# Two output blocks of a decoder layer as seven block products, with the weight sums formed in memory by DMA

## The chip, the cores and the metric

The kernel runs on one core of one Trainium2 chip. The metric is device time of one execution in microseconds (us); the time of a kernel is the median of its runs. A profile is of one execution, and its span is somewhat shorter than that execution's time.

The core has a matrix engine (TensorE, PE in the profile; its weight loads are listed as PEld), a vector engine (VectorE, DVE), a scalar engine (ScalarE, ACT), a general engine (GpSimd, POOL) and a sync engine (SP) that issues DMAs. PE reads on-chip buffers and writes accumulators in PSUM, of which there are eight banks of 128 x 512 float32. DMAs move data between the memory outside the core and the buffers, and also from one place of that memory to another; those that POOL issues can add to what lies at their destination.

## The reference, cut to what matters

One layer of a hybrid decoder, float32, 256 tokens of width 2048, one batch:

```python
h = rms_norm(x, ln1_g)
proj = h @ w_in                                   # 2048 x 14416, cut into twelve parts
o_attn = dsa_attention(...)                       # sparse attention over the top 64 keys
o_ret = silu(rg) * group_norm_heads(retention)    # retention branch, its output gated
merged = sigmoid(ga) * (o_attn @ w_up_attn) + sigmoid(gb) * (o_ret @ w_up_ret)
x = x + merged @ w_out                            # all four of these matrices 2048 wide
h2 = rms_norm(x, ln2_g)
x = x + square(relu(h2 @ w_ff1)) @ w_ff2          # 2048 -> 8192 -> 2048
```

The change concerns `merged @ w_out`: 256 x 2048 by 2048 x 2048.

## The kernel before, in words

**Precision.** PE multiplies in a reduced float32 format. Every operand is therefore split in two, a rounded high part and the low rest, and each product is three matmuls: high by high, high by low, low by high (`products`, L438, L439, L440). For weights the split is made on the fly: ACT copies the raw tile to the high part `whi` (L379), DVE subtracts to get the low part `wlo` (L380).

**Tiles.** The 256 tokens are two row tiles (T = 2) of 128. The contraction of 2048 is 16 tiles of 128. A weight matrix is worked in column blocks of 512 (BN). A plain block is 16 x 2 x 3 = 96 matmuls into two PSUM banks, and is called by its name: UR0 to UR3 (`w_up_ret`), O0 to O3 (`w_out`), F1 (`w_ff1`). Weights are loaded as tiles of four contraction tiles (KC = 4) by 512 columns, 1 MB each, by DMAs of SP (L333), and split in halves of two (HC = 2). One such half is an *item*: a load tile gives two items. A plain item is 12 matmuls.

**Products.** In some stages two column blocks are formed together as a 2 x 2 block product with seven multiplications in place of eight (Strassen in Winograd's form, `strassen`, `PRODUCTS`, `ORDER`): the two row tiles by the two contraction halves against the weight's quarters A, B, C, D. An item of a product has six matmuls. X11 and X12 are the first row tile's two contraction halves, X21 and X22 the second's; G5, G6, G3 and G7 are differences of them, called forms, made once. The sums of weight quarters (A+B, B+C and so on) are added by DVE in the loaded tiles (L367, lists `SUMS` and `GATE_SUMS`), a few by an adding DMA of POOL (`GATE_ADDS`, L387). After product 4 of the numbering DVE combines the partial results (L712). Before the change this is done for the gates' blocks (`gates`, woven with plain blocks) and for the feed-forward groups (`merged`), not for `w_out`.

**Order.** `program()` lists all items in the order in which PE works them, and `stream()` the weights in memory. `ahead(i)` runs at item i: it issues loads whose first use lies up to eight items ahead (LOAD_AHEAD) and splits two or three items ahead. The loaded tiles go through a ring of four buffers (`raw`); quarters of products have two more (`rawb`), and in some stages there is a second ring (`rawc`). Side work (norms, transposes, gating) is written as generators in the list `work`, which `step()` advances once per contraction tile or item and `drain()` empties. A scheduler then fixes each engine's order ahead of the run, by priority in program order and by its own estimates; at run time each engine goes through its list in order and waits on semaphores.

**PSUM banks.** `deal` hands out the eight banks: `pm` for plain blocks, `pq` for products, `pt` for transposes, `pa` for the rest. From the retention stage to F1 it is pm 4, pt 2, pa 2; for the feed-forward groups pf 4, pq 3, pt 1.

**The stage around the change.** UR0 and UR1 are worked side by side, then UR2, then UR3. `merge` multiplies each block by its gate and adds the attention branch (L951, L952), `merged_in` transposes the result on PE (L467) and splits it into `mT`, the stationary operand of the output blocks. After UR3 everything is drained. Blocks O0 to O3 follow one after another. When one is done, DVE adds the residual x into `x2` (L1033), ACT forms the sum of squares (L1035) and stores the sums by DMA (L1036). After O2 the inverse root of the first three columns' mean square is formed (DVE, and POOL for the power, L450), and `next_norm` takes columns 0, 1 and 2 through scaling (ACT, L993), transposes (PE, L1001), a copy with the gain into `xr` (ACT, L1003) and the split into `xf` (ACT L985, DVE L986), while O3 runs. F1's two blocks then read `xf` in the order of columns 0 to 3; column 3 and the forms for the feed-forward groups (`forms`, L1013) are made beside them.

Of the kernel before, what the change touches and what calls it, by code (L numbers as in the profile page):

```python
# [17 lines left out]
P = 128  # L18
# [60 lines left out]
def stream():  # L79
# [22 lines left out]
    b += [(("O", i), "w_out", 0, DK, i * BN, BN) for i in range(4)]  # L102
# [28 lines left out]
def block(key):  # L131

    return [(key, h, s) for h in range(DK // KC) for s in range(KC // HC)]
# [16 lines left out]
def program():  # L150
# [8 lines left out]
    for key in [("UR", 2), ("UR", 3)] + [("O", i) for i in range(4)] + [("F1", i) for i in (1, 0)]:  # L159
        out += block(key)  # L160
# [20 lines left out]
def block_kernel(ctx, tc, cst, rot, xt, gains, w, x, ret_gn_g, ret_gn_b, out):  # L181
# [89 lines left out]
    at, B, off = {}, {}, 0  # L271
    for key, name, _, nk, _, n in stream():
        B[key] = (nk, n)
        for h in range(nk // KC):
            src = w[off:off + KC * P * n].rearrange("(p c n) -> p c n", p=P, c=KC)
            if key in BESIDE:
# [5 lines left out]
    use = program()  # L282

    def tile_of(item):
        if item[0] == "Q":
            return (PRODUCTS[ORDER[item[2]]][1], item[1], item[3]), 0
# [4 lines left out]
    def sum_of(item):  # L291

        if item[0] == "Q":
# [103 lines left out]
    def ahead(i):  # L397
        for _ in range(2):
# [16 lines left out]
    def run_blocks(keys, act, before=None):  # L415
# [3 lines left out]
        for k0 in range(0, nk, HC):  # L419
            for key, p in zip(keys, ps):  # L420
                n = B[key][1]
                ws = weights((key, k0 // KC, k0 % KC // HC))
                for c in range(HC):
# [4 lines left out]
                    products(p, [z[:, c, :n] for z in ws], [act(k, t) for t in range(T)], k == 0, k == nk - 1)  # L428
        return [[z[:, :B[key][1]] for z in p] for key, p in zip(keys, ps)]

    def run_block(key, act, before=None):
        return run_blocks([key], act, before)[0]
# [262 lines left out]
    def strassen(item):  # L695
# [4 lines left out]
        p = ORDER[n]  # L700
# [243 lines left out]
    def merged_in(i, t, m):  # L944
        yield from transpose_in(mT, 4 * i, t, m)
# [11 lines left out]
    for i in range(2):  # L957
        merge(i, both_ps[i])
    work.append(branches(2))
    for i in (2, 3):  # L960
        ps = run_block(("UR", i), of(rT))
        if i == 2:
            drain()
        merge(i, ps)
# [5 lines left out]
    drain()  # L970
    ex.release()
# [3 lines left out]
    late["f2"] = ctx.enter_context(tc.tile_pool(name="f2", bufs=1, side="right", reuse_waits="tile"))  # L975
# [3 lines left out]
    xf = late["f1"].tile([P, 2, len(PRODUCTS), HK, P], F32R, tag="xf", name="xf")  # L979
    xr = [late["f2"].tile([P, T, HK, P], F32, tag="rawb", name=nm("xr"), bufs=2) for _ in range(2)]  # L980
# [48 lines left out]
    for i in range(4):  # L1029
        ps = run_block(("O", i), of(mT))  # L1030
        for t in range(T):
            z = x2[:, t, i * BN:(i + 1) * BN]
            nc.vector.tensor_tensor(z, ps[t], z, op=ALU.add)  # L1033
            junk = stage()
            nc.scalar.activation(junk, z, AF.Square, accum_out=ss2[:, 4 * t + i:4 * t + i + 1])  # L1035
            nc.scalar.dma_start(sums[:, t, i * BN:(i + 1) * BN], z)  # L1036
        if i == 2:

            ss = small(T)
            nc.vector.tensor_reduce(ss, ss2.rearrange("p (t i) -> p t i", t=T)[:, :, :3], axis=AX.X, op=ALU.add)  # L1040
            rs = cp.tile([P, T], F32, name="rs")
            nc.vector.tensor_copy(rs, rsqrt(ss, T, 1.0 / (3 * BN)))
            work.append(z for k in range(3) for z in next_norm(k))
# [4 lines left out]
    def norm_end():  # L1048
        yield from next_norm(3)
# [24 lines left out]
    for i in (1, 0):  # L1074
        ps = run_block(("F1", i), lambda k, t: form(quads[k // HK][t], k % HK))
# [87 lines left out]
```

## Time and profile before

| what | value |
|---|---|
| runs | 1606.47 us median of 3 (1606.38 to 1606.73) |
| profiled execution, its time | 1606.29 us |
| its span | 1604.3 us, 19728 instructions |
| DMA traffic | 368.57 MB, 230 GB/s in the mean |
| DVE, ACT, POOL busy | 81%, 63%, 8% of the span |
| granted PE clock | full in all 40 slices |

How to read the lines: in the timeline a line has the start and length in us, the engine, the kernel's line, the operation, output and inputs with their shapes, and in brackets the idle time before it and what ended it. Matmuls overlap, so that a matmul's own length is longer than the distance to the next one. In the windows a line has a stretch, its length, and for PE, PEld, DVE, ACT and POOL the busy us with the number of instructions, then the granted clock, the mean busy share of the 16 DMA engines and GB/s. A line of DMA issues has the tensors, the queue, the count, KB each and the median us from issue to landing. A queue's line has packets, MB and the share of 16 engines' time.

### The profile page before, as it was taken

How to read it: one execution, taken by the hardware profiler on the slowest of the kernel's cores; microseconds unless marked ns; L12 is line 12 of the kernel's file. 1: busy time of each engine (PE TensorE's matmuls, PEld its weight loads, DVE VectorE, ACT ScalarE, POOL GpSimd, SP SyncE). 2: the span in 40 equal slices, each digit the busy share in tenths (PEclk: the TensorE clock that was granted, in tenths of full speed). 3: DMA queues.
4: the chain of work that ended last, by engine and by line, in shares of the span. 5: the costliest groups of instructions: out<-in, count | busy, mean ns of one | idle time of the engine just before them, and what ended most of it. 6: DMA issues, size and time to landing. Idle time of an engine off the chain costs nothing.

```text
span 1604.3 us, 19728 instructions
## 1 busy us (share of the span) xinstructions
PE 1597.7 (100%) x7394; PEld 1327.8 (83%) x7394; DVE 1298.9 (81%) x1354; ACT 1017.4 (63%) x1262; POOL 126.5 (8%) x169
## 2 busy tenths in 40 slices
PE   9999999999999999999999999999999999999998
PEld 8978888888888888888888888888888888888887
DVE  6578777998989899677765579898989898989884
ACT  7555567666766666454444666767767776767672
POOL 0000001010000001112210000000000000000000
PEclk9999999999999999999999999999999999999999
DMA  9645348978878684765766574767676767777673
GB/s 331 220 146 186 135 153 305 299 266 274 258 287 266 230 258 176 285 222 195 265 250 250 194 277 149 257 194 246 204 260 200 242 213 236 236 236 236 216 205 130
DMA packets 75759, 368.57 MB, mean 230 GB/s; under 512 B 8592, under 2 KB 15376, under 8 KB 42512
## 3 DMA queue, kind: packets, MB, share of 16 engines
q1 hardware_dynamic: 56224, 311.32, 53.0%
q0 software_dynamic: 16704, 49.82, 14.3%
q10 hardware_dynamic: 2736, 6.18, 1.0%
q8 instruction: 58, 0.95, 0.2%
q14 instruction: 37, 0.30, 0.1%
HBM read 337.92 MB, written 29.36 MB: 229 GB/s over the span
## 4 chain that ended last, share of the span: by engine, by line
PE 97%; DVE 2%; ACT 0%; issue 0%; DVEq 0%
PE pm L439 14%; PE pm L440 14%; PE pm L438 14%; PE pq L438 9%; PE pq L439 9%; PE pq L440 9%; PE pf L438 7%; PE pf L439 7%; PE pf L440 7%; PE pt L467 1%; DVE wlo L380 1%; DVE mid L593 1%; PE pa L438 0%; PE pa L439 0%; PE pa L440 0%; PE pa L264 0%
## 5 line engine op out<-in xcount | busy, mean ns | idle before, releaser
L380 DVE TENSOR_TENSOR wlo<-raw,whi 128x1024 fp32r<-128x1024 f32 (+2 forms) x556 | 659.7, 1200 | 206.1 <-ACT whi L379 197.9
L379 ACT ACTIVATE whi<-raw 128x1024 fp32r<-128x1024 f32 (+2 forms) x556 | 576.0, 1043 | 382.3 <-PE pm L440 233.9
L438 PE MATMUL pm<-whi,act 128*128 128x512 f32 (+1 forms) x992 | 384.7, 388 | 0.0
L439 PE MATMUL pm<-wlo,act 128*128 128x512 f32 (+1 forms) x992 | 381.8, 385 | 0.5 <-DVE wlo L380 0.5
L440 PE MATMUL pm<-whi,act 128*128 128x512 f32 (+1 forms) x992 | 381.4, 384 | 0.0
L380 DVE TENSOR_TENSOR wlo<-rawc,whi 128x1024 fp32r<-128x1024 f32 x176 | 214.7, 1220 | 42.2 <-ACT whi L379 40.4
L379 ACT ACTIVATE whi<-rawc 128x1024 fp32r<-128x1024 f32 x176 | 186.6, 1060 | 85.7 <-PE pf L440 23.2
L439 PEld LDWEIGHTS pm<-wlo,act 128*128 128x128 f32 x992 | 186.4, 188 | 35.9 <-DVE wlo L380 3.0
L440 PEld LDWEIGHTS pm<-whi,act 128*128 128x128 f32 x992 | 186.2, 188 | 35.1
L438 PEld LDWEIGHTS pm<-whi,act 128*128 128x128 f32 x992 | 186.4, 188 | 33.9 <-issue 0.3
L438 PE MATMUL pf<-whi,act 128*128 128x512 f32 x512 | 200.0, 391 | 0.0
L439 PE MATMUL pf<-wlo,act 128*128 128x512 f32 x512 | 199.4, 390 | 0.0
L440 PE MATMUL pf<-whi,act 128*128 128x512 f32 x512 | 199.4, 389 | 0.0
L367 DVE TENSOR_TENSOR raw<-raw,raw 128x2048 f32<-128x2048 f32 x86 | 196.6, 2286 | 0.8
L438 PE MATMUL pq<-whi,xf 128*128 128x512 f32 x392 | 154.3, 394 | 0.0
L439 PE MATMUL pq<-wlo,xf 128*128 128x512 f32 x392 | 152.8, 390 | 0.0
L440 PE MATMUL pq<-whi,xf 128*128 128x512 f32 x392 | 152.8, 390 | 0.0
L440 PEld LDWEIGHTS pf<-whi,act 128*128 128x128 f32 x512 | 96.1, 188 | 20.1
L438 PEld LDWEIGHTS pf<-whi,act 128*128 128x128 f32 x512 | 96.0, 188 | 20.1 <-ACT whi L379 0.4
L439 PEld LDWEIGHTS pf<-wlo,act 128*128 128x128 f32 x512 | 96.1, 188 | 19.7
L1109 POOL DMA_DIRECT2D sums<-ev x56 | 49.1, 969 | 580.8 <-ACT ev L1108 579.9
L440 PEld LDWEIGHTS pq<-whi,xf 128*128 128x128 f32 x392 | 73.6, 188 | 15.3
(206 smaller groups left out, 1623.2 us busy)
## 6 DMA issues: line engine op xcount, KB each, us to landing
raw<-in_w_dram SPq DMA_DIRECT2D x188, 1024.0 KB, 6.1
rawc<-in_w_dram SPq DMA_DIRECT2D x56, 1024.0 KB, 6.3
rawc<-in_w_dram SPq DMA_DIRECT2D x64, 512.0 KB, 5.9
sums<-ev POOLq DMA_DIRECT2D x56, 256.0 KB, 5.5
raw<-in_w_dram POOLq DMA_DIRECT2D x10, 1024.0 KB, 9.9
raw<-in_w_dram SPq DMA_DIRECT2D x8, 736.0 KB, 5.0
raw<-in_w_dram SPq DMA_DIRECT2D x7, 512.0 KB, 7.9
raw<-in_w_dram SPq DMA_DIRECT2D x8, 368.0 KB, 7.8
```

The lines of the kernel that those rows point to most:

```text
L367: nc.vector.tensor_tensor(one, one, two, op=ALU.add)
L379: nc.scalar.activation(a, src, AF.Copy)
L380: nc.vector.tensor_tensor(b, src, a.bitcast(F32), op=ALU.subtract)
L438: nc.tensor.matmul(d, h, hi, start=first, stop=False, skip_group_check=skip)
L439: nc.tensor.matmul(d, h, lo, start=False, stop=False, skip_group_check=skip)
L440: nc.tensor.matmul(d, l, hi, start=False, stop=last, skip_group_check=skip)
L467: nc.tensor.transpose(ps[:, c * P:(c + 1) * P], src[:, c * P:(c + 1) * P], ident)
L593: nc.vector.scalar_tensor_tensor(sc[t], src, iw[:, t, h:h + 1], sc[t], op0=ALU.mult, op1=ALU.add)
L1109: nc.gpsimd.dma_start(sums[:, t, i * BN:(i + 1) * BN], z, accum_op=ALU.add)
```

## The change

O0 and O1 (columns 0 and 1 of 512) become one unit `OUT` of seven products in the order `OUT_ORDER`. Its 28 items are woven by `second_half` with plain items: the first eight (X11 by A, then G7 by B's sum) with UR3's eight, then four items of O2 alone, then the other 20 with the remaining twelve items of O2 and O3, two for three; the last two items stand alone. `program` uses that order in place of UR2, UR3, O0 to O3.

The sums of `w_out`'s quarters are made in memory. Four tensors `pre` receive copies of the quarters by DMAs that SP issues at items 24, 27, ... 45, and sums by adding DMAs that POOL issues at items 46, 49, 54, 57, 62, 65, 70, 73, 1 MB each; both are issued in `ahead`. The products load from `pre` or from the weights through the ordinary ring of four buffers, and no sum is added on DVE for them.

The banks are dealt as pm 4, pq 3, pt 1 already after UR1. `merged_in` copies each transposed tile a second time, into `xr`, from which `m_forms` makes G7 after UR1, and G5, G6 and G3 after UR3. When columns 2 and 1 are both done, the norm starts from those two, and F1's first block reads the columns in the order 2, 1, 3, 0 (`NORM_COLS`); columns 3 and 0 follow beside it.

```diff
     b += [(("UR", i), "w_up_ret", 0, DK, i * BN, BN) for i in range(4)]
-    b += [(("O", i), "w_out", 0, DK, i * BN, BN) for i in range(4)]
+    quarters(OUT, "w_out", 0)
+    b += [(("O", i), "w_out", 0, DK, i * BN, BN) for i in (2, 3)]
...
+OUT = ("O", 0)
+OUT_ORDER = (0, 2, 5, 1, 3, 4, 6)
+NORM_COLS = (2, 1, 3, 0)
...
+def second_half():
+    q = [("Q", OUT, n, h, s) for n in range(len(OUT_ORDER)) for h in range(HK // KC) for s in range(KC // HC)]
+    a, b = q[:8], q[8:]
+    out = block(("UR", 2))
+    for x, y in zip(block(("UR", 3)), a):
+        out += [x, y]
+    two = block(("O", 2)) + block(("O", 3))
+    out, two = out + two[:4], two[4:]
+    n, j = len(b) - 2, 0
+    for i, x in enumerate(b):
+        out.append(x)
+        while j < len(two) and j * n < (i + 1) * len(two):
+            out.append(two[j])
+            j += 1
...
+    pre = {z: dp.tile([HK // KC, P, KC * BN + 16], F32, name=nm("pre"))[:, :, :KC * BN].rearrange(...) for z in QUARTERS}
+    for n, p in enumerate(OUT_ORDER):
+        z = PRODUCTS[p][1]
+        for h in range(HK // KC):
+            at[("OQ", n), h] = (pre[z][h] if p in (1, 2, 4, 6) else base[z, h], BN)
+    for j, (z, two) in enumerate((("A", "B"), ("B", "C"), ("C", "A"), ("D", "C"))):
+        for h in range(HK // KC):
+            background[24 + 6 * j + 3 * h] = (pre[z][h], base[z, h], False)
+            background[46 + 8 * j + 3 * h] = (pre[z][h], base[two, h] if j < 2 else pre[two][h], True)
...
     def ahead(i):
+        if i in background:
+            d, a, add = background[i]
+            if add:
+                nc.gpsimd.dma_start(d, a, accum_op=ALU.add)
+            else:
+                nc.sync.dma_start(d, a)
...
     def merged_in(i, t, m):
-        yield from transpose_in(mT, 4 * i, t, m)
+        yield
+        yield
+        ps = psum_t()
+        for c in range(4):
+            nc.tensor.transpose(ps[:, c * P:(c + 1) * P], m[:, c * P:(c + 1) * P], ident)
+        split_into(mT, 4 * i, 4, t, ps)
+        half, c0 = divmod(4 * i, HK)
+        nc.scalar.activation(xr[half][:, t, c0:c0 + 4, :], ps.rearrange("p (c i) -> p c i", c=4), AF.Copy)
         moved[0] += 1
...
+    ex.release()
+    deal(pm=4, pq=3, pt=1)
...
+    def m_forms():
+        while moved[0] < 2 * T:
+            yield
+        for c in (0, 4):
...
+        while moved[0] < 4 * T:
+            yield
+        for f, d, one, two in ((G5, x22, x21, x22), (G6, x11, x11, x22), (G3, x12, x12, x11)):
+            hi, lo = (mx["xf"][:, a, f] for a in range(2))
+            nc.vector.tensor_tensor(d, one, two, op=ALU.subtract)
+            nc.scalar.activation(hi, d, AF.Copy)
+            yield
+            nc.vector.tensor_tensor(lo, d, hi.bitcast(F32), op=ALU.subtract)
+            yield
...
-    for i in range(4):
-        ps = run_block(("O", i), of(mT))
...
+    while rest:
+        item = rest.pop(0)
+        if item[0] == "Q":
+            strassen(item)
+        else:
+            ps = plain(item, of(mT))
+            for t in range(T if ps else 0):
+                out_block(item[0][1], t, ps[t])
+        if not started and all((i, t) in done for i in NORM_COLS[:2] for t in range(T)):
+            started = True
+            work.append(first_norms())
...
     for i in (1, 0):
-        ps = run_block(("F1", i), lambda k, t: form(quads[k // HK][t], k % HK))
+        ps = run_block(("F1", i), lambda k, t: form(quads[k // HK][t], k % HK), order=NORM_COLS if i else range(DK // KC))
```

`out_block` does what stood in the loop over O0 to O3 (L1033, L1035, L1036) for one block and row tile; `first_norms` does the norm of columns 2 and 1 after the inverse root over those two.

More of the change, by code (lines that the diff above doesn't have):

```diff
@@ L413, in weights, with run_blocks @@
         return parts.pop(i)
-    def run_blocks(keys, act, before=None):
+    def run_blocks(keys, act, before=None, order=range(DK // KC)):
         nk = B[keys[0]][0]
         ps = [[psum("pm") for _ in range(T)] for _ in keys]
-        for k0 in range(0, nk, HC):
+        ks = [h * KC + k for h in order for k in range(0, KC, HC)]
+        for k0 in ks:
             for key, p in zip(keys, ps):
@@ new lines, in plain, with out_block @@
+    def plain(item, act):
+        (key, i), h, s = item
+        ws = weights(item)
+        if (h, s) == (0, 0):
+            acc[key, i] = [psum("pm") for _ in range(T)]
+        for c in range(HC):
+            step()
+            k = h * KC + s * HC + c
+            products(acc[key, i], [z[:, c] for z in ws], [act(k, t) for t in range(T)], k == 0, k == DK - 1)
+        return acc.pop((key, i)) if k == DK - 1 else None
+    done = set()
+    def out_block(i, t, src):
+        z = x2[:, t, i * BN:(i + 1) * BN]
+        nc.vector.tensor_tensor(z, src, z, op=ALU.add)
+        junk = stage()
+        nc.scalar.activation(junk, z, AF.Square, accum_out=ss2[:, 4 * t + i:4 * t + i + 1])
+        nc.scalar.dma_start(sums[:, t, i * BN:(i + 1) * BN], z)
+        done.add((i, t))
@@ new lines, in block_kernel @@
+    work.append(branches(2))
+    work.append(m_forms())
+    blocks[OUT] = {"form": m_form, "finish": lambda u, t, i, dst, src: out_block(i, t, src), "b": {}, "e": {}}
+    rest = second_half()
+    while rest[0][0] != ("O", 2):
+        item = rest.pop(0)
+        if item[0] == "Q":
+            strassen(item)
+            continue
+        ps = plain(item, of(rT))
+        if ps:
+            if item[0][1] == 2:
+                while moved[0] < T * 2 or any(z.gi_frame is not None and z.__name__ == "branches" for z in work):
+                    step()
+            merge(item[0][1], ps)
@@ L1027, in forms, with first_norms @@
         late["g7"] = xr[0][:, 1:2]
-    for i in range(4):
-        ps = run_block(("O", i), of(mT))
[L1031 to L1043, printed above, removed]
+    rs = cp.tile([P, T], F32, name="rs")
+    def first_norms():
+        lo, n = min(NORM_COLS[:2]), 2
+        ss = small(T)
+        nc.vector.tensor_reduce(ss, ss2.rearrange("p (t i) -> p t i", t=T)[:, :, lo:lo + n], axis=AX.X, op=ALU.add)
+        nc.vector.tensor_copy(rs, rsqrt(ss, T, 1.0 / (n * BN)))
+        for k in NORM_COLS[:2]:
+            yield from next_norm(k)
+    started = False
+    while rest:
+        item = rest.pop(0)
+        if item[0] == "Q":
+            strassen(item)
+        else:
[5 more added lines that the diff above has]
+            work.append(first_norms())
     drain()
@@ L1048, in norm_end @@
     def norm_end():
[L1049 removed]
+        for k in NORM_COLS[2:]:
+            yield from next_norm(k)
         yield from forms()
```

66 lines of the change are left out of this document (45 added, 21 removed).

## The prediction

> **What bounds the kernel now.** I read the page first: busy time, then the chain that ended last.
>
> ```profile
> span 1604.3 us, 19728 instructions
> ...
> PE 1597.7 (100%) x7394; PEld 1327.8 (83%) x7394; DVE 1298.9 (81%) x1354; ACT 1017.4 (63%) x1262; POOL 126.5 (8%) x169
> ...
> PE 97%; DVE 2%; ACT 0%; issue 0%; DVEq 0%
> ```
>
> PE (TensorE) is busy all the time and is 97% of the chain: work taken off PE is worth its own length, unless another engine fails to feed the stage that is left. The profiled execution took 1606.29 us, 1.99 more than its span; the median of the runs is 0.18 above that. A measurement of this kernel tells about 0.2%, 3.2 us, from no change.
>
> A matmul's row says 0.39 us, but matmuls overlap. The price of one is the distance of starts, and the best row for it is a whole block: the adds (L1033) that take blocks O0, O1, O2, O3 out of PSUM, from the timeline of VectorE (DVE).
>
> ```profile
> 855.04 1.23 DVE L380 TENSOR_TENSOR wlo<-raw,whi 128x1024 fp32r<-128x1024 f32 x1 [1.50 <-ACT whi L379]
> 856.19 1.28 DVE L1033 TENSOR_TENSOR x<-pm,x 128x512 f32<-128x512 f32 x2
> ...
> 877.95 1.28 DVE L1033 TENSOR_TENSOR x<-pm,x 128x512 f32<-128x512 f32 x2
> ...
> 899.71 1.28 DVE L1033 TENSOR_TENSOR x<-pm,x 128x512 f32<-128x512 f32 x2
> ...
> 908.81 1.29 DVE L986 TENSOR_TENSOR xf<-xr,xf 128x512 fp32r<-128x512 f32 x2 [1.35 <-ACT xf L985]
> ...
> 914.44 1.29 DVE L986 TENSOR_TENSOR xf<-xr,xf 128x512 fp32r<-128x512 f32 x2
> ...
> 924.41 0.68 DVE L1033 TENSOR_TENSOR x<-pm,x 128x512 f32<-128x512 f32 x1
> ```
>
> O1 and O2 each take 21.76 us for 96 matmuls (16 contraction tiles, 2 row tiles, 3 products of the hi/lo split): 0.2267 us a matmul. O3 takes 24.70: the 2.94 more are 24 transposes of three norm columns, 0.98 a column.
>
> **The change, part by part.** *Two output blocks as seven products.* Before: 2 x 96 = 192 matmuls. After: 7 products x 8 contraction tiles x 3 = 168. Less 24 x 0.2267 = **5.44 us of PE**, all on the chain. The number of transposes stays the same.
>
> *More weight splits.* Each item (two contraction tiles) still needs one ACT copy and one DVE subtract, and a product item carries 6 matmuls instead of 12: 28 items replace 16, so 12 x 1.06 us more on ACT (L379) and 12 x 1.23 on DVE (L380). No weight sums are added on DVE, since memory holds them. The fullest part is from UR3's end to the fourth product: 19 items, 9 of them product items, 174 matmuls, 39.5 us of PE. DVE there: 19 splits and three forms of two operations (128x1024 like a split) at 1.23, 4 merge operations, 2 low parts and 3 output adds (128x512 like L1033) at 0.64: 36.5 of 39.5 us, 92%. The stage that compares is the gates' (products woven with plain blocks too), in the windows:
>
> ```profile
> 57.75:116.46 58.71, 58.71 (x335) 50.89 (x333) 37.86 (x63) 31.77 (x44) 0.00 (x0) 1.00 0.50 174
> 119.63:211.32 91.69, 91.69 (x453) 75.44 (x453) 75.05 (x142) 54.52 (x104) 4.91 (x3) 1.00 0.45 160
> 330.00:540.00 210.00, 210.00 (x929) 172.99 (x928) 192.39 (x166) 143.89 (x152) 18.41 (x30) 1.00 0.82 273
> 840.00:860.00 20.00, 20.00 (x90) 16.57 (x89) 10.55 (x10) 9.21 (x12) 0.00 (x0) 1.00 0.78 308
> 900.00:920.00 20.00, 20.00 (x101) 16.41 (x100) 11.20 (x15) 18.37 (x35) 0.72 (x1) 1.00 0.49 172
> ```
>
> At 330 to 540 DVE is at 192.39 of 210 us, 92%, and PE loses nothing. So 0 below; above, the 1.5 that 1% of this 125 us stretch would be. I take **+0.3**, near the row that compares.
>
> *Evictions and forms.* Per UR block two more ACT copies into xr, the forms of G7, G5, G6, G3 and one product's copies: ACT is at 9.21 of 20 us in that stretch (840 to 860), so nothing; should ACT fill up, it is the end of the stretch, below.
>
> *One transpose bank (pt) instead of two, from UR2 on.* The four merged tiles of UR0 and UR1 become ready together and now pass one bank in turn. PE's order puts transposes where their bank is free, and matmuls of UR2 stand between. After UR3 the old kernel emptied everything before O0:
>
> ```profile
> 835.26 0.39 PE L439 MATMUL pm<-wlo,act 128*128 128x512 f32 x1
> 835.50 1.15 PE L467 MATMUL pt<-csb,got 128*128 128x128 f32 x8
> 836.41 0.48 PE L440 MATMUL pm<-whi,act 128*128 128x512 f32 x1
> ```
>
> The 8 transposes take 0.91 us from start to start, no more than O3's (2.94 for 24, 0.98 for 8). PE lost nothing at that seam, so weaving UR3 with products gains nothing there: **0**. Should a transpose come to stand with its bank still full, PE loses one eviction, under 2 us; the nearest row is this one.
>
> *Entry of F1.* Before, the norm of columns 0 to 2 runs in O3, with 24.70 us of cover, and F1 starts on ready operands. After, columns 2 and 1 start when product 6 of 7 ends (call it T0) and F1 reads column 2 first. The old chain runs from O2's add at 899.71 to the first low part of the norm, 908.81 + 0.64: 9.74 us. ACT's part of it:
>
> ```profile
> 901.16 0.61 ACT L1035 ACTIVATE stg<-x 128x512 f32<-128x512 f32 x1
> 901.67 0.19 ACT L1035 ACTIVATION_READ_ACCUMULATOR stg<-x 128x1 f32 x1
> ...
> 903.91 1.34 ACT L993 ACTIVATE stg<-x,rs 128x512 f32<-128x512 f32 x2 [1.44 <-DVE rs L1042]
> 905.16 1.04 ACT L379 ACTIVATE whi<-raw 128x1024 fp32r<-128x1024 f32 x1
> 906.11 1.54 ACT L1003 ACTIVATE xr<-pt,gT 128x256 f32<-128x256 f32 x4
> ...
> 908.14 1.16 ACT L985 ACTIVATE xf<-xr 128x512 fp32r<-128x512 f32 x2
> ```
>
> The new chain has four product sums ahead (in `strassen`, of L1033's shape, 0.64 each), 2.6, and with one pt bank the second half of the transposes waits for two xr copies, 0.77: 13.1 us. Cover after T0: two O3 items (24 matmuls), four product items (24), 8 transposes: 10.88 + 0.98 = 11.86. Short by 1.3. The lower bound is 0 (the splits that I left in the chain may run elsewhere); a gain is excluded, since PE had no gap here before. For the upper one, add up ACT from T0 to F1's last column: four norm columns at 1.34 + 1.54 + 1.16 = 4.04, five squares at 0.80, ten splits at 1.06 = 30.8 us, against 48 + 72 matmuls and 32 transposes of PE, 31.1: full, where before it reached 18.37 of 20 without loss. With the 1.44 wait and a split in front of a norm step twice that is some 4 us. I take **+1.5**, by the chain. The later columns come 5.6 us apart (908.81, 914.44), F1 uses one per 5.44 + 0.98: no more loss.
>
> *Sums in memory.* Eight 1 MB copies, memory to memory, go into the SP queue at items 24 to 45, and eight adding DMAs into the POOL queue at items 46 to 73. Their times come by counting the L379 rows of ACT, one an item; shown are items 24, 25, 45, 46, 65 and 73:
>
> ```profile
> 57.75 0.82 ACT L379 ACTIVATE whi<-raw 128x736 fp32r<-128x736 f32 x1 [1.18 <-PE pm L440]
> 59.75 0.82 ACT L379 ACTIVATE whi<-raw 128x736 fp32r<-128x736 f32 x1 [1.18 <-PE pm L440]
> ...
> 116.46 1.06 ACT L379 ACTIVATE whi<-raw 128x1024 fp32r<-128x1024 f32 x1 [1.66 <-PE pm L440]
> ...
> 119.63 1.06 ACT L379 ACTIVATE whi<-raw 128x1024 fp32r<-128x1024 f32 x1 [2.11 <-PE pm L440]
> ...
> 182.53 1.06 ACT L379 ACTIVATE whi<-raw 128x1024 fp32r<-128x1024 f32 x1 [0.99 <-PE pm L440]
> ...
> 211.32 1.06 ACT L379 ACTIVATE whi<-raw 128x1024 fp32r<-128x1024 f32 x1 [1.06 <-PE pm L440]
> ```
>
> The issuing is hidden: SP has no compute, and POOL is busy 4.91 of 91.69 us there. Copies wait for nothing; what queues behind them is the loads. No trace here has a memory-to-memory DMA. The page gives what its queues took of the 16 engines, and landing times:
>
> ```profile
> q1 hardware_dynamic: 56224, 311.32, 53.0%
> q0 software_dynamic: 16704, 49.82, 14.3%
> ...
> sums<-ev POOLq DMA_DIRECT2D x56, 256.0 KB, 5.5
> raw<-in_w_dram POOLq DMA_DIRECT2D x10, 1024.0 KB, 9.9
> raw<-in_w_dram SPq DMA_DIRECT2D x8, 736.0 KB, 5.0
> ```
>
> SP's loads: 0.530 x 1604.3 / 311.32 = 2.73 us per MB. A copy lies between 2.73 (as a load) and 5.46 (read and write apart): 22 to 44 us in 58.7 us whose DMA share is 0.50, that is 29 busy. Total 51 to 73. At the upper end loads behind a copy run 14 us late. A load goes out seven items before its split (four raw buffers, two items each), 14 us at the 2.00 pace of item 24, less 5.0 to land: 9 us of slack, more at the later pace of 3.17, and splits run two items ahead of PE. Price 0 to 5 us; nearest row is the load, so **0**.
>
> The Trainium skill, "DMA: Bandwidth & Descriptors", section "Issuing engines are not separate DMA queues", says that DMAs of all issuers share the same 16 engines and interleave, so that no queue is a free path; its "Latency and other measured facts" gives 214 GB/s as the full rate of copies between HBM tensors. That makes an estimate of 4.9 us a copy and 68 us in all, 10 over the window; the sum would stay as it is, as that is inside the slack, and no run so far shows such a copy.
>
> *Sum.* 1606.29 - 5.44 + 0.3 + 1.5 = 1602.65; at the median **1602.8**.
>
> **The rivals.**
> *All of it comes through* (F1's entry hidden): 1601.0 to 1601.9. For it: PE loses nothing before at 92% of ACT. Against it: the chain of 13.1 us.
> *F1's entry eats the gain*: ACT full, +4 there and up to 1.5 in the weave: 1606.3, with a spread from 1604.
> *Late copies*: up to +5 by the upper price, 1607.8 at most. Against it: the share of 0.50 and 9 us of slack.
> *Four raw buffers starve the weave.* The seven products load 14 MB where two plain blocks loaded 8, and the 57 us weave takes 15 loads (one per 3.8 us) through four buffers. A buffer is held for the landing and, by my estimate, 5.5 us more: the issue, and from its first split to the end of its second with a neighbour's item between (1.36 or 2.72 us of PE, 1.06 + 1.23 for the split). It decides from a landing of 4 x 3.8 - 5.5 = 9.7 us on. Rows of the windows 330 to 540 and 840 to 920:
>
> ```profile
> raw<-in_w_dram SPq DMA_DIRECT2D x24, 1024.0 KB, 7.3
> ...
> raw<-in_w_dram SPq DMA_DIRECT2D x14, 1024.0 KB, 4.8
> ```
>
> At 11.5 us each tile comes 0.45 late: 6.8 us, 1609.5. Against it: 7.3 is the worst stage's.
> *Slower: adds that hold POOL.* The last two adds (items 70, 73) read what those of items 62 and 65 wrote, and POOL waits in order; behind them stands the power step of the last head norm, whose query tiles PE needs:
>
> ```profile
> 221.44 1.64 POOL L450 TENSOR_TENSOR small<-small,half 128x8 f32<-128x8 f32 x1 [27.16 <-DVE small L449]
> ```
>
> The sixth add starts at 182.53 at the latest; if adds run one after another from 119.63, it has landed at 119.63 + 6d. Up to d = 16.9 us nothing waits. Bounds: 9.9 us (1 MB added into a buffer) and 22 (four times the 5.5 of 256 KB added into memory). At d = 20 the step is 18 us late, and the attention behind it: 1621. Against it: 22 counts the fixed part of the landing four times, and d is 4.6 us by the page's queue share (0.143 x 1604.3 / 49.82), twice that with the write.
>
> **How the numbers follow.** Forecast 0.42 (own range 1601.9 to 1604), all through 0.17, F1's entry 0.19, late copies 0.06, raw buffers 0.08, POOL 0.08. Faster than 1603.3: all through and 0.34 of the forecast, 0.51. Slower than 1609.7: POOL and most of the raw buffers, 0.14. The rest, 0.35, is the same. The range 1600.5 to 1608 holds the first four cases, 0.84; its low end is the full 5.44 with half a microsecond for the spread of runs.
>
> **What would show it.** Right: UR2's start to F1's first matmul shorter by some 3.6 us, with PE idle only ahead of F1's first operands, released by DVE L986 of column 2; the loads of 58 to 220 us land by 10 us and PE runs there as before; the adds land in under 17 us. Wrong: PE waiting on weight parts (wlo) inside the weave with ACT waiting on a DMA (raw buffers); a later start of the first RV block (copies, POOL); F1's columns each late (ACT).

## The result, and the profile after

The changed kernel takes 1623.39 us (four runs, 1623.27 to 1623.46), the kernel before 1606.43 (four runs, 1606.29 to 1606.73): a ratio of 1.0105, interval 1.0089 to 1.0121, 17 us slower where 1602.8 was forecast. The page of the changed kernel, in the order of the parts shown of before:

```profile
span 1621.4 us, 19799 instructions
...
PE 1602.0 (99%) x7370; PEld 1328.1 (82%) x7370; DVE 1326.5 (82%) x1381; ACT 1039.9 (64%) x1290; POOL 132.6 (8%) x177
...
q1 hardware_dynamic: 58240, 326.00, 54.4%
q0 software_dynamic: 17856, 58.21, 16.6%
...
PE 92%; DVE 3%; DMA 3%; ACT 1%; issue 1%; POOL 0%; DVEq 0%; ACTq 0%
```

PE runs 24 matmuls fewer (7370 for 7394), but is busy longer, 1602.0 for 1597.7 us. Its share of the chain fell from 97 to 92%, and DMA, which had none, has 3%. So there are new waits, some of them for transfers, and the matmuls that are left are partly slower.

**Where: first the front.** VectorE's and GpSimd's timelines give landmarks. The fourth power step of the head norms, which was at 221.44, is late by 12.07 us. GpSimd (POOL) in the changed kernel:

```profile
56.73 1.06 POOL L445 DMA_DIRECT2D pre<-in_w_dram  x1 [5.94 <-DMA pre<-in_w_dram]
...
136.14 0.81 POOL L445 DMA_DIRECT2D pre<-pre  x1 [13.41 <-DMA pre<-in_w_dram]
148.17 1.66 POOL L501 TENSOR_TENSOR small<-small,half 128x8 f32<-128x8 f32 x1 [11.21 <-DVE small L500]
...
233.51 1.64 POOL L501 TENSOR_TENSOR small<-small,half 128x8 f32<-128x8 f32 x1 [27.16 <-DVE small L500]
```

L445 is the adding DMA. All eight go out at 56.73 to 136.14, ahead of the first of the four head norms' power steps (148.17), each as soon as what it works on has landed; the items that the code names for them (46 to 73) run from 119.63 to 211.32 in the kernel before. Their place in the text was not their place in POOL's order: the scheduler put these adds, which wait for DMAs alone, ahead of power steps that wait for VectorE. What that does to the 16 DMA engines stands in the windows (the last three columns: granted clock, DMA share, GB/s), first of the kernel before, then of the changed one:

```profile
60.00:75.00 15.00, 15.00 (x92) 15.00 (x91) 6.63 (x8) 7.51 (x10) 0.00 (x0) 1.00 0.73 252
83.00:130.00 47.00, 46.84 (x243) 36.62 (x241) 39.02 (x100) 23.27 (x30) 0.00 (x0) 1.00 0.40 137
130.00:148.00 18.00, 18.00 (x92) 14.97 (x91) 13.35 (x20) 9.93 (x12) 1.64 (x1) 1.00 0.63 229
```

```profile
60.00:75.00 15.00, 13.84 (x84) 13.53 (x82) 4.63 (x5) 4.93 (x7) 0.82 (x1) 1.00 1.03 258
83.00:130.00 47.00, 46.84 (x249) 36.97 (x247) 35.88 (x82) 23.35 (x33) 3.42 (x4) 1.00 1.02 319
130.00:148.00 18.00, 14.35 (x48) 10.39 (x47) 12.57 (x31) 7.21 (x10) 0.81 (x1) 0.81 1.02 326
```

The DMA views from 50 to 130 us, again first before, then changed:

```profile
raw<-in_w_dram SPq DMA_DIRECT2D x12, 1024.0 KB, 4.8
```

```profile
raw<-in_w_dram SPq DMA_DIRECT2D x11, 1024.0 KB, 16.8
pre<-in_w_dram SPq DMA_DIRECT2D x8, 1024.0 KB, 17.9
pre<-in_w_dram POOLq DMA_DIRECT2D x4, 1024.0 KB, 12.1
pre<-pre POOLq DMA_DIRECT2D x3, 1024.0 KB, 14.4
```

The DMA share is full (1.02 and 1.03) where the kernel before has 0.73, 0.40 and 0.63, and a weight load lands in 16.8 us, not 4.8. ScalarE then waits for a load, and PE for ScalarE:

```profile
138.22 2.00 ACT L423 ACTIVATE whi<-raw 128x1024 fp32r<-128x1024 f32 x2 [7.20 <-DMA raw<-in_w_dram]
```

```profile
136.67 0.39 PE L491 MATMUL pm<-whi,act 128*128 128x512 f32 x1
139.32 0.64 PE L489 MATMUL pm<-whi,act 128*128 128x512 f32 x1 [2.26 <-ACT whi L423]
140.58 0.79 PE L490 MATMUL pm<-wlo,act 128*128 128x512 f32 x1 [0.62 <-DVE wlo L424]
141.18 0.63 PE L491 MATMUL pm<-whi,act 128*128 128x512 f32 x1
141.60 0.63 PE L489 MATMUL pm<-whi,act 128*128 128x512 f32 x1
```

Two such stretches and one short wait make 7.6 us of gaps (2.33 + 0.79, 1.03, 2.42 + 1.03; a gap here is the distance of two starts less 0.2267 us a matmul, 0.165 at 368 columns). The other 4.5 us are nearly all slow starts. Behind the second stretch, from the last lines shown up to 146.29, starts are 0.427 us apart, not 0.227; behind the first, from 78.36 to 81.42, they are 0.306 apart, not 0.165. The Trainium skill, "TensorE: Matmul & The Clock Gate", section "What's actually happening", describes a clock gate that goes to half rate after an idle window and opens again after about 3.4 us of work; the trace agrees in kind, with starts 0.427 us apart for about 5 us. Its section "Why this matters for your kernels" asks for no idle gaps over about 3 us; here 2.42 and 1.03 close together were enough.

**Second, the weave.** One gap of 2.62 us. PE, and VectorE ahead of it:

```profile
875.36 0.39 PE L489 MATMUL pq<-whi,act 128*128 128x512 f32 x1
878.21 0.50 PE L490 MATMUL pm<-wlo,act 128*128 128x512 f32 x1 [2.46 <-DVE wlo L424]
```

```profile
873.12 1.23 DVE L1053 TENSOR_TENSOR xf<-xr,xf 128x1024 fp32r<-128x1024 f32 x1 [1.79 <-ACT xf L1051]
874.26 1.22 DVE L1050 TENSOR_TENSOR xr<-xr,xr 128x1024 f32<-128x1024 f32 x1
875.79 1.23 DVE L1053 TENSOR_TENSOR xf<-xr,xf 128x1024 fp32r<-128x1024 f32 x1 [0.32 <-ACT xf L1051]
876.93 1.22 DVE L424 TENSOR_TENSOR wlo<-raw,whi 128x1024 fp32r<-128x1024 f32 x1
```

L1050 and L1053 are the forms G5, G6, G3. Three of their operations, which no matmul reads before 885.82, stand in VectorE's order ahead of the split (L424) that PE is waiting for.

**Third, F1's entry.** PE, then VectorE:

```profile
931.83 0.39 PE L491 MATMUL pq<-whi,act 128*128 128x512 f32 x1
933.41 0.33 PE L1127 MATMUL pt<-csb,stg 128*128 128x128 f32 x1 [1.19 <-ACT stg L1119]
934.02 0.55 PE L1127 MATMUL pt<-csb,stg 128*128 128x128 f32 x3 [0.29 <-ACT stg L1119]
935.50 1.11 PE L1127 MATMUL pt<-csb,stg 128*128 128x128 f32 x4 [0.93 <-ACT xr L1129]
937.54 1.11 PE L1127 MATMUL pt<-csb,stg 128*128 128x128 f32 x4 [0.93 <-ACT xr L1129]
938.67 0.80 PE L489 MATMUL pm<-whi,xf 128*128 128x512 f32 x1
...
939.69 0.63 PE L489 MATMUL pm<-whi,xf 128*128 128x512 f32 x1
940.11 0.63 PE L491 MATMUL pm<-whi,xf 128*128 128x512 f32 x1
```

```profile
922.26 0.68 DVE L763 TENSOR_TENSOR stg<-pq,stg 128x512 f32<-128x512 f32 x1
922.86 1.22 DVE L424 TENSOR_TENSOR wlo<-raw,whi 128x1024 fp32r<-128x1024 f32 x1
...
925.79 1.29 DVE L1074 TENSOR_TENSOR x<-stg,x 128x512 f32<-128x512 f32 x2
926.99 2.36 DVE L424 TENSOR_TENSOR wlo<-raw,whi 128x1024 fp32r<-128x1024 f32 x2
...
932.43 0.17 DVE L1162 COPY rs<-small 128x2 f32<-128x2 f32 x1 [0.61 <-POOL small L501]
...
938.65 1.29 DVE L1112 TENSOR_TENSOR xf<-xr,xf 128x512 fp32r<-128x512 f32 x2 [3.72 <-ACT xf L1111]
```

From 931.83 to 938.67 PE does twelve small transposes; 5.2 us of this are gaps, and starts 0.43 us apart behind it cost 1.5 more.

The sum: 12.07 in front. From 770 to 1015 us all distances of PE's starts beyond the pitch (what a matmul of that width takes from start to start at the usual rate, 0.2267 us at 512 columns) make 10.85, where the kernel before has 0.48 from 770 to 1000; with the 5.44 saved, 12.07 + 10.37 - 5.44 = 17.0, and 16.96 was measured.

### The profile page after: what moved, and what is told of

It is laid out like the page before. It is cut to its first block, busy times and chain, and to the rows that moved or that the text cites. A ratio compares the mean times of both kernels' runs of the same rounds, so it can differ in the third digit from the quotient of the medians.

```text
span 1621.4 us, 19799 instructions
## 1 busy us (share of the span) xinstructions
PE 1602.0 (99%) x7370; PEld 1328.1 (82%) x7370; DVE 1326.5 (82%) x1381; ACT 1039.9 (64%) x1290; POOL 132.6 (8%) x177
## 4 chain that ended last, share of the span: by engine, by line
PE 92%; DVE 3%; DMA 3%; ACT 1%; issue 1%; POOL 0%; DVEq 0%; ACTq 0%
PE pm L490 12%; PE pm L491 12%; PE pm L489 12%; PE pq L491 10%; PE pq L490 10%; PE pq L489 10%; PE pf L489 7%; PE pf L491 7%; PE pf L490 7%; DMA raw<-in_w_dram 3%; DVE wlo L424 1%; PE pt L518 1%; ACT whi L423 0%; PE pa L489 0%; PE pa L490 0%
## 5 line engine op out<-in xcount | busy, mean ns | idle before, releaser
L424 DVE TENSOR_TENSOR wlo<-raw,whi 128x1024 fp32r<-128x1024 f32 (+2 forms) x568 | 675.1, 1204 | 186.9 <-ACT whi L423 177.3
L423 ACT ACTIVATE whi<-raw 128x1024 fp32r<-128x1024 f32 (+2 forms) x568 | 588.1, 1043 | 370.8 <-PE pm L491 194.9
L489 PE MATMUL pm<-whi,act 128*128 128x512 f32 (+1 forms) x928 | 361.3, 390 | 4.4 <-ACT whi L423 4.4
L490 PE MATMUL pm<-wlo,act 128*128 128x512 f32 (+1 forms) x928 | 358.8, 387 | 4.8 <-DVE wlo L424 4.8
L491 PE MATMUL pm<-whi,act 128*128 128x512 f32 (+1 forms) x928 | 358.3, 386 | 0.0
L424 DVE TENSOR_TENSOR wlo<-rawc,whi 128x1024 fp32r<-128x1024 f32 x176 | 215.1, 1222 | 41.4 <-ACT whi L423 39.5
L490 PEld LDWEIGHTS pm<-wlo,act 128*128 128x128 f32 x928 | 175.6, 189 | 38.8 <-DVE wlo L424 8.0
L489 PEld LDWEIGHTS pm<-whi,act 128*128 128x128 f32 x928 | 175.5, 189 | 37.1 <-ACT whi L423 5.8
L491 PEld LDWEIGHTS pm<-whi,act 128*128 128x128 f32 x928 | 175.5, 189 | 33.0
L489 PE MATMUL pq<-whi,xf 128*128 128x512 f32 x416 | 163.6, 393 | 0.0
L491 PE MATMUL pq<-whi,xf 128*128 128x512 f32 x416 | 162.1, 390 | 0.0
L490 PE MATMUL pq<-wlo,xf 128*128 128x512 f32 x416 | 162.0, 389 | 0.0
L490 PEld LDWEIGHTS pf<-wlo,act 128*128 128x128 f32 x512 | 96.1, 188 | 19.7
L491 PEld LDWEIGHTS pq<-whi,xf 128*128 128x128 f32 x416 | 78.1, 188 | 16.2
```

The lines of the kernel that those rows point to most:

```text
L423: nc.scalar.activation(a, src, AF.Copy)
L424: nc.vector.tensor_tensor(b, src, a.bitcast(F32), op=ALU.subtract)
L489: nc.tensor.matmul(d, h, hi, start=first, stop=False, skip_group_check=skip)
L490: nc.tensor.matmul(d, h, lo, start=False, stop=False, skip_group_check=skip)
L491: nc.tensor.matmul(d, l, hi, start=False, stop=last, skip_group_check=skip)
```

## The experiments

All times are medians, and the edits shown are abridged. The ratio is against the kernel before on the same chip (1606.7 to 1607.0 us). "Lost" is the sum of the distances of PE's starts beyond the pitch from 770 to 1000 us. The third column has the profiled execution's own time less the 1606.29 of before, and beside it what the parts make: lost, less 0.48, less the 5.44 saved, and the power step less 221.44. In all 18 runs the two agree within 0.6 us, so that no part of the time is missing and the saving is there each time. (A profiled execution can be off its median, most for the early first norm, by 3.6 us.)

| kernel | time, ratio (interval) | profiled execution / by sum | lost | power step at |
|---|---|---|---|---|
| no sums | 1614.71, 1.0049 (1.0034 to 1.0064) | +8.4 / +8.4 | 13.5 | 222.25 |
| copies only | 1612.78, 1.0038 (1.0023 to 1.0053) | +7.3 / +6.9 | 12.6 | 221.71 |
| adds held | 1612.60, 1.0038 (1.0023 to 1.0053) | +5.9 / +5.9 | 11.6 | 221.66 |
| early first norm | 1622.39, 1.0095 (1.0078 to 1.0112) | +19.7 / +19.4 | 12.7 | 233.99 |
| held, forms spread | 1609.93, 1.0019 (1.0010 to 1.0027) | +3.6 / +4.2 | 9.7 | 221.84 |
| held, O3's end alone | 1610.18, 1.0018 (1.0009 to 1.0027) | +4.0 / +4.0 | 9.6 | 221.83 |
| held, both ("base") | 1606.50, 0.9999 (0.9990 to 1.0007) | +1.6 / +2.1 | 7.5 | 221.98 |
| base, six items at the end | 1607.05, 1.0002 (0.9993 to 1.0011) | +0.7 / +0.4 | 6.3 | 221.47 |
| base, two pt banks | 1605.76, 0.9993 (0.9984 to 1.0002) | -0.6 / -0.9 | 5.0 | 221.55 |
| base, splits first | 1610.72, 1.0025 (1.0015 to 1.0034) | +4.4 / +4.6 | 10.2 | 221.72 |
| base, both of these | 1611.52, 1.0030 (1.0020 to 1.0040) | +5.1 / +4.5 | 9.8 | 222.13 |
| the same, six items | 1609.95, 1.0020 (1.0012 to 1.0029) | +3.3 / +3.3 | 9.2 | 221.43 |
| two pt, forms on POOL | 1616.23, 1.0055 (1.0042 to 1.0067) | +9.9 / +10.3 | 15.9 | 221.78 |
| two pt, UR3 alone | 1605.81, 0.9993 (0.9984 to 1.0002) | -0.2 / -0.3 | 5.6 | 221.40 |
| UR3 alone, forms on POOL | 1617.58, 1.0064 (1.0051 to 1.0077) | +8.6 / +9.0 | 14.3 | 222.07 |
| two pt, three split buffers | 1609.22, 1.0014 (1.0005 to 1.0023) | +4.3 / +4.5 | 10.2 | 221.59 |
| UR3 alone, banks 4, 3, 1 | 1607.43, 1.0005 (0.9996 to 1.0013) | +0.8 / +1.0 | 6.9 | 221.47 |
| UR3 alone, banks 3, 3, 2 | 1604.27, 0.9985 (0.9976 to 0.9994) | -2.0 / -2.1 | 3.7 | 221.49 |

**The front: which of the DMAs.** Three runs. The first leaves the sums out of the computation, the second the adds.

```
- background[24 + ...] = (pre[z][h], base[z, h], False)     # no sums: both lines out
- background[46 + ...] = (pre[z][h], ..., True)             # copies only: this one out
+ background[52 + ...] = (pre[z][h], ..., True)             # adds held: items 52 to 79, and
+ with tc.issue_after(last_pow): nc.gpsimd.dma_start(d, a, accum_op=ALU.add)   # adds held
```

> Leaves out the copies and the adding DMAs; the products read the plain weight quarters, so the weight sums are missing from the output. Theory: the eight copies and eight adds fill the DMA engines between 50 and 140 us, loads land late there, PE waits and then runs at a lower clock; that is 12.0 of the loss, so 1611.4 us, with PE unbroken from 60 to 160 us. Rival: the early gaps only move work that would wait later anyway, or reading the sums in the weave is what costs: 1618 or more.

> Keeps the eight copies and leaves out the eight adds; the products read unsummed copies. Theory (adds needed for the collision): by the queue shares of before and after, an add takes some 4.7 us of all engines per MB and a copy 2 to 3, so copies alone leave the engines under full: 1611 to 1612. Rival (copies alone delay the loads behind them in SP's queue, the price I had put at up to 5 us): 1613 to 1617.

> All of the change, but the adds are queued on POOL in pairs behind the power steps of the four head norms (about 137, 163, 192 and 221 us of the old timeline), where the text of the change had put them; nothing is left out. Theory: the scheduler's moving of the adds to 57 to 136 us makes the collision, and there is room for them later (DMA share 0.45): 1611 to 1612. Rival (an add costs the loads as much wherever it stands, or POOL waiting for a copy holds back a power step): 1618 or more.

The power step is back at 222 in all three. With the adds held behind the head norms' power steps on POOL, all of the work is done and the 12 us in front are gone. The times did not fall as far as expected: the run without sums came out 3.3 us above its theory, the other two 0.6 to 0.8, since all three lose more from 770 us on (the column "lost") than the changed kernel did. In the run without sums, waits ahead of the merged transposes are 1.1 us longer there, and slow starts cost 2.4 us in place of 1.0. GpSimd and the windows of the run with the adds held:

```profile
221.66 1.66 POOL L503 TENSOR_TENSOR small<-small,half 128x8 f32<-128x8 f32 x1 [25.45 <-DVE small L502]
223.29 1.71 POOL L447 DMA_DIRECT2D pre<-pre  x2
```

```profile
60.00:75.00 15.00, 15.00 (x92) 15.00 (x91) 6.47 (x7) 7.70 (x10) 0.00 (x0) 1.00 0.96 359
83.00:130.00 47.00, 46.85 (x244) 36.66 (x242) 39.03 (x98) 23.28 (x30) 0.00 (x0) 1.00 0.64 233
130.00:148.00 18.00, 18.00 (x92) 14.99 (x91) 13.35 (x21) 9.94 (x12) 3.51 (x3) 1.00 0.89 267
```

The copies stay, with a DMA share up to 0.96, and PE is busy as before. So the cause of the 12 us is shown: the adds beside the copies and loads. Copies without adds do not bring it, nor do the same adds later on.

**F1's entry: start the norm earlier.** The first norm takes column 2 alone (as soon as O2 is done), column 1 follows; the adds stay early.

```
- lo, n = min(NORM_COLS[:2]), 2
+ lo, n = NORM_COLS[0], 1          # column 1: work.append(next_norm(1)) when it is done
```

> The change with the first norm made from column 2 alone as soon as O2 is done, and column 1 when it is done; the scale that the norm uses is undone exactly later. Nothing is left out. Theory: the entry of F1 costs 6.8 us because the chain of column 2 starts only when product 6 of 7 is done; with column 2 ready long before, 5 to 6 us come back: 1617.5 to 1618.5. Rival: ACT is full from there to F1's last column (31 us of work against 31 us of PE), so that the wait moves to the next columns: 1621 to 1623.

The gaps at the entry fell from 5.2 to 2.01 and 0.81, and PE there waits for F1's own weight split, which stands behind norm steps and squares on ScalarE; slow starts and the 0.62 that came in the weave took part of it back. The time fell by 1 us, the rival's number, not the 5 to 6 expected. The trace can't account for this 1 us: its execution is 3.6 us above the median, with 1.6 us more of waits ahead of the merged transposes.

**Weave and entry apart.** On top of the held adds:

```
  formed.add(f)
- yield
+ for _ in range(4): yield                                    # forms spread (G5, G6, G3)
- out, two = out + two[:4], two[4:]
+ out, two, end = out + two[:4], two[4:12], two[12:]          # O3's end alone:
- return out                                                  # (six items: two[4:10], two[10:])
+ return out + end
- NORM_COLS = (2, 1, 3, 0)
+ NORM_COLS = (2, 1, 0, 3)                                    # with O3's end
```

> The adds queued behind the head norms, as in the run that held them (1612.6 us), and beside that only the forms G7, G5, G6 and G3 of the merged rows spread out: four steps instead of one between two of them. The sums stay as they are. Theory: the gap of 2.61 us at 863.70 stands there because two forms lie ahead of a needed weight split in the order of VectorE; spread out, it goes, and with it nothing else: about 1610.0 us, F1's entry as wide as before (about 5 us of gaps and a slowed clock). Rival: VectorE and ScalarE are full in that stretch, so that the wait only moves to another split: 1612.6.

> Held adds; the last four items of O3 (48 matmuls, 10.9 us of TensorE) are taken out of the weave and stand alone behind the seventh product, and the norm takes the columns in the order 2, 1, 0, 3, since column 3 now comes last. Same work. Theory: F1's entry is a chain of 18.1 us with 11.9 us of cover; with 10.9 us more cover the loss of 6.8 us goes, and the time falls from 1612.6 to about 1606; the gap at 863.70 stays. Rival one: ScalarE is full from the sixth product on, whatever stands on TensorE, so the gaps come back in other places: 1611 to 1613. Rival two: the denser weave (20 product items over 8 plain ones) starves on VectorE, which goes from 30 of 41 us to about 25 of 30: 0 to 3 us lost there, 1606 to 1609.

> Held adds, spread forms and the four items of O3 at the end, together. Theory: the three losses are separate and add up, so all that is left is the saving of 5.4 us against 0.7 us of gaps ahead of transposes: 1602 to 1603.5 us. Rival: ScalarE and VectorE are full, so one loss takes the other's place: 1606 to 1610.

> As the one before, with the last six items of O3 at the end instead of four (16.3 us of TensorE). Theory: if F1's entry is already covered by four items, nothing more is won: the same within 1 us. If four are too few, this is faster by what was left. Rival: the weave of 20 product items over 6 plain ones (192 matmuls, 43.5 us) starves on VectorE (28 us of splits less 2.5, and some 12 us of sums): 1 to 3 us slower.

Spread forms: 2.7 us faster, the gap at 863.70 gone and F1's entry as it was; the theory, to 0.1 us. O3's end alone: the gaps at F1's entry fell from 5.1 to 1.3 us, but the weave, now denser, lost 1.17 + 1.22 where 2.61 had been and 0.78 + 0.81 further on, so 2.4 us came back of the 6.8 expected; the mechanism of its second rival, and more of it than that had (1606 to 1609). Both together came to 1606.5, inside the rival's range (1606 to 1610) and 3 us above the theory's upper end. With six items F1's entry has only 0.48 left, and the weave 1.40 more: no change. F1's loss is thus mostly a question of cover; what is left is short waits, most of them for weight parts.

**The weave's short waits.** Two remedies on the base:

```
- deal(pm=4, pq=3, pt=1)
+ deal(pm=4, pq=2, pt=2)                                      # two pt banks
- if first_gate - 16 <= i <= last_gate:
+ if first_gate - 16 <= i <= last_gate or (UR3's first item) <= i <= (O2's last):   # splits first
```

> The run with held adds, spread forms and four items of O3 at the end (1606.5 us), with the eight PSUM banks of this stretch dealt as 4 pm, 2 pq, 2 pt instead of 4, 3, 1: transposes get the second bank back that the change took from them, the products lose one of three. Theory: the gaps of 0.43, 1.10 and 0.51 us ahead of the transposes of merged_in (792 to 820) go, since they wait for the copy that empties the one bank: 1604.5 us. Rival: two product banks are too few, a product then waits for the sums of the one before last: new gaps ahead of pq matmuls and 1606 to 1609.

> The same base (1606.5 us), with the weight splits from UR3 to the end of O2 given priority in the engines' order, as the gates have it. Theory: the gaps of 0.94 and 0.80 us ahead of wlo matmuls (866.86, 882.29) stand because forms and sums lie ahead of splits; with the splits first they go: 1604.8 us. Rival: the splits wait for their own buffers, and a form that comes later holds a product up: no change, or up to 2 us slower.

> Two transpose banks and the splits first, on the same base. Theory: both effects add, and little but the saved matmuls is left: 1602.8 to 1603.5 us. Rival: two product banks starve the products: not under 1606.

> As the one before, with six items of O3 at the end instead of four, where F1's entry showed no gap at all. Theory: the 0.81 us ahead of F1's own operands (936.02) goes too: 1602 to 1603 us. Rival: the weave of 20 product items over 6 plain ones is bound by VectorE (1.40 us lost there at 902.38 with six items): within 0.7 us of the one before.

With two transpose banks the gaps of 0.43, 1.10 and 0.51 us ahead of the merged transposes are gone, as expected; 0.48 ahead of a product (waiting for the sum that empties its bank) came instead. Its time stands at 0.7 us under the base, across two comparisons, where the theory had 2. Splits first was a miss: 4.2 us slower than the base, beyond the rival's 2. With the splits ahead, VectorE is busy without a break from 863.70 to 884.88; three operations of forms come close together at 873.92 to 879.06, and PE waits 3.75 us for a split (882.53) that stands behind them, two other splits and two sums. With two transpose banks as well, forms at 872.56 and 873.69 stand ahead of a product's sum, for which PE waits 3.96; that time is the rival's (not under 1606), and six items at the end win back 1.6, which neither expectation had. This speaks for an even order on VectorE and against a priority; no run tests it by itself.

**Single operations or buffers?** The prediction had compared the weave with the gates' stage, which loses nothing at 92% of VectorE. But there the split parts have a fourth buffer (`late["fourth"]`); from UR2 to UR3's end they have three, until F1's pool opens (`late["f1"]`).

```
- nc.vector.tensor_tensor(d, one, two, op=ALU.subtract)       # the forms' first step
+ nc.gpsimd.tensor_tensor(d, one, two, op=ALU.subtract)       # forms on POOL
- a, b = q[:8], q[8:]
+ a, b = [], q                                                # UR3 alone
- (late["f1"], 1) if "f1" in late and i % 4 == 3
+ (late["f1"], 1) if (F1 has started) and i % 4 == 3          # three split buffers
- while next_split[0] < min(len(use), i + SPLIT_AHEAD + ("f1" in late or ...) + 1):
+ while next_split[0] < min(len(use), i + SPLIT_AHEAD + ((F1 has started) or ...) + 1):
```

> The run with two transpose banks (1605.8 us), with the five subtractions that form the merged operands (128x1024, 1.22 us each on VectorE) on GpSimd, which is idle there. Theory one (a form ahead of a split on VectorE makes the short waits): the gap of 1.27 us at 867.73 goes and the time falls to about 1604.5. Theory two (too few buffers of split parts): the splits wait as before, 1605.8; forms on GpSimd take 2 to 3 us each, so a product may wait for one instead, up to 1607.

> The run with two transpose banks (1605.8 us), with UR3 left alone and all 28 product items woven with O2 and O3, where the split parts have four buffers instead of three. Same work. Theory two (buffers): the waits of 1.27 and 0.48 us at 867 to 872 go, 1604 us. Theory one (single operations of VectorE): the forms now meet the same items elsewhere, the waits move: 1605 to 1607. A third possibility: 28 product items over 12 plain ones fill VectorE (49 us of splits and some 17 of forms and sums against 71 of TensorE), with 1 to 2 us of new waits.

> UR3 alone and the forms' subtractions on GpSimd. Theory one and two both expect the least waiting of all here: 1602.5 to 1604 us. If it is not under 1605, neither the forms nor the buffers are what is left.

> The run with two transpose banks (1605.8 us), with the fourth buffer of split parts withheld until F1 starts, so that the whole weave has three. Theory two: a product item lasts 1.36 us and a split 1.06 + 1.23 us after its buffer is free, so with three buffers the waits multiply: 1610 us or more. Theory one: buffers hardly matter at 73% of VectorE: 1606 to 1607.

Three buffers in the whole weave: 3.5 us slower than four, where the theory of buffers had 4 or more and the other none or 1. (The run also starts the splits one item later, as three buffers need; the two go together.) With UR3 alone the waits of 1.27 and 0.48 at 867 to 872 are gone; two waits for product banks took their place, so the time is the same. That is the number of the theory of single operations, but what PE waits for there are sums that empty banks:

```profile
875.34 0.47 PE L490 MATMUL pq<-whi,xf 128*128 128x512 f32 x1 [0.88 <-DVE x L1076]
...
904.63 0.47 PE L490 MATMUL pq<-whi,act 128*128 128x512 f32 x1 [1.74 <-DVE stg L764]
```

Forms on POOL missed by both theories, 10 and 12 us slower. VectorE, then GpSimd, then ScalarE of the first of them:

```profile
861.24 6.48 DVE L425 TENSOR_TENSOR wlo<-raw,whi 128x1024 fp32r<-128x1024 f32 x2 [0.21 <-ACT whi L424]
```

```profile
798.07 1.30 POOL L1042 TENSOR_TENSOR stg<-xr 128x512 f32<-128x512 f32 x1
...
860.34 9.63 POOL L1052 TENSOR_TENSOR xr<-xr,xr 128x1024 f32<-128x1024 f32 x3 [51.61 <-ACT xr L1005]
```

```profile
806.11 0.63 ACT L1043 ACTIVATE stg<-stg 128x512 fp32r<-128x512 f32 x1 [4.16 <-POOL stg L1042]
```

While GpSimd subtracts, two splits on VectorE take 6.48 us instead of 2.35. And two subtractions of the form G7 (798.07 is the first) stand among the gate products of UR2's merge in POOL's order. ScalarE, which rounds their results, waits 4.05 and 4.16 us for them, with its copies of weights queued behind; at 800 to 810 PE has 5.6 us of gaps, waiting for weight parts (4.9 in the other run with forms on POOL), that no run without forms on POOL has.

**Banks by stage.** UR3 alone, with the banks dealt as before the change up to its end (4 pm, 2 pt, 2 pa), then anew:

```
- deal(pm=4, pq=2, pt=2)                 # after UR1
+ deal(pm=4, pq=3, pt=1)                 # after UR3; the other run: deal(pm=3, pq=3, pt=2)
```

> The run with UR3 alone (1605.8 us, banks 4, 2, 2), with the banks dealt as before the change (4 pm, 2 pt, 2 pa) until UR3's end, and 4 pm, 3 pq, 1 pt from there. Theory (what is left are waits for PSUM banks): the waits of 1.03 and 1.91 us for product sums go, some 0.8 us ahead of F1's operands comes back with the one transpose bank: 1603 to 1604 us, which is faster than before by 3 to 4 us. Rival: with three product banks the items run closer and the waits turn to weight parts: 1605 to 1606.

> As the one before, but 3 pm, 3 pq, 2 pt from UR3's end. Theory: F1's entry has its second transpose bank, so 0.8 us less than the one before: 1602.5 to 1603.5 us. Rival: with three plain banks O3's second row tile waits for the sum that empties O2's, and F1's for O3's: 0.7 to 1.4 us each, 1604 to 1606.

With one transpose bank it was a miss, beyond the rival (1605 to 1606), whose waits for weight parts are there: 1.06, 0.99 and 1.19. With two, and three plain banks, 1604.27: faster than before by 0.15% (interval 0.06 to 0.24%). That is 0.8 us above the theory's top and in the rival's range (1604 to 1606), but the rival's waits of plain products for sums are not in the trace. It is also the best of 18 kernels, and 2.4 us is under the 3.2 that the prediction takes a measurement to tell, so the gain is small and thinly shown. PE is busy 1593.2 us in it; the largest gap left:

```profile
906.73 0.61 PE L490 MATMUL pm<-whi,act 128*128 128x512 f32 x2
908.37 0.51 PE L491 MATMUL pm<-wlo,act 128*128 128x512 f32 x1 [1.03 <-DVE wlo L424]
```

Why the single transpose bank also brings the waits for weight parts at 854 to 857 is open.

## Why the prediction was wrong, point by point

*Sums in memory: the step that failed.* It took the adds to run at items 46 to 73, beyond the copies, because the code names these items, and priced copies and adds in windows of their own. In their place the runs showed adds at 56.73 to 136.14, in the copies' window, and 12.07 us. This alone does not make the miss: with the adds held, 1612.60 is still above the range, by the two terms below. The queues' shares were a fair guide to the sizes: by the page of the changed kernel, q0 took 0.166 x 1621.4 - 0.143 x 1604.3 = 39.7 us more, 5.0 an add (4.6 to 9.2 was said), and they landed in 12.1 to 14.4 us (under 17). Copies: q1 took 0.544 x 1621.4 - 0.530 x 1604.3 = 31.8 us more; less 6.3 MB of added weight loads at 2.73 that is 14.6, 1.8 a copy. The same sum gives 1.5 to 2.9 in the other runs with copies, and 2.8 where the adds are left out, so a copy is near the lower bound of 2.73; and alone copies cost nothing, as said. The sizes were right; adding them up over the same 90 us, from 50 to 140, would have shown the collision: loads that took a share of 0.54 before (48.6 us), 40 of adds and 15 to 22 of copies are 103 us at least. The rival of late copies (up to +5) was the right place and the wrong culprit. The rival of adds that hold POOL came nearest in number (1621), by luck: POOL's order as such held no power step up, as the one at 148.17 waits for VectorE, not for an add.

*F1's entry: mis-sized, 1.5 for 6.7.* The chain of 13.1 us was 18.1 (from the sixth product's end at 921.2, where its last sum starts 1.06 later, to the low part at 938.65 + 0.65). The stretch from the first sum to rs, priced at 4.2 + 2.6, took 10.2 (922.26 to 932.43), since four splits of weights, 4.8 us, stand between the sums in VectorE's order. The rest, 6.9, was as priced (6.3). Then there are the slow starts, 1.5 us, which no term had. The rival in which F1's entry eats the gain had +4 here, for a full ScalarE; the run of the early norm, where PE waits for a copy on ScalarE instead, is in line with its reasoning. How much of the 6.7 is ScalarE's and how much VectorE's is not separated.

*Weave: mis-sized, 0.3 for 2.6 and more.* The share of VectorE (92% in the gates) was the wrong measure: the waits are single operations ahead of a split, with VectorE at 41.50 of the 55 us from 866 to 921 in the changed kernel (75%), and up to UR3's end the weave had one buffer of split parts less than the stage compared. Raw buffers did not starve the weave: from 840 to 920 its loads land in 5.2 and 5.9 us, and ScalarE waits for none.

*One transpose bank: 0 for 0.7 to 2.* The bound of two microseconds an eviction held; the row chosen did not.

*Matmuls saved: right.* 24 fewer, and in every run the time follows from 5.44 less the listed losses.

## What to carry to other kernels

Work "in the background" can end up elsewhere in its engine's order than the text names: look up or force its place (here behind a power step on its queue) and add up every transfer of that window before pricing the first. A share of busy time does not tell whether a short chain is covered: list what stands between its steps on each engine, and count the buffers that the split parts turn in. Where PE has a gap of 2 us with another close by, allow for slow starts behind it (here 1.5 to 2.8 us a time).

## What the hardware showed that was not expected

- Of all 16 engines, an adding DMA of 1024 KB within memory took 5.0 us by the queues' shares (4.6 to 5.2 over the runs with adds), and a plain copy 1.5 to 2.9; a load takes 2.73 per MB.
- After gaps of 2.42 and 1.03 us close together PE's starts were 0.427 us apart for some 5 us; a single gap of 2.6 us was followed by the usual distance (878.21 on) in the changed kernel, but by the slow one in the two runs without adds (868.01 on without sums, 867.66 on with copies only).
- GpSimd and VectorE slowed each other: a subtraction of 128x1024 took 3.21 us on GpSimd (9.63 for three), and a split on VectorE 3.24 instead of 1.18. The Trainium skill, "SBUF — State Buffer", section "SBUF: two separate sides", says that the two share a pair of ports as an exclusive lock, also for a VectorE operation with two SBUF inputs against a GpSimd one that reads SBUF; the rows agree: three subtractions at twice the 1.28 us of a 128x512 operation on GpSimd and two splits at 1.18, one after the other, would be 10.0 us, and the three took 9.63.
